# A two-layer hybrid decoder trunk: sixteen weight rests formed by adding DMAs instead of VectorE

## The chip, the cores and the metric

The kernel runs on one core of one Trainium2 chip. The metric is the device time of one execution in microseconds; the time before is the median of three runs. All views of the profile come from one profiled execution.

## The reference

The reference is a decoder trunk of two layers over 512 tokens of width 1024, in float32.

```
for i in range(2):
    h = rms_norm(x, mix_norm[i])
    if i == 0:  x = x + attention_and_short_conv(h)      # one input, one output projection
    else:       x = x + gla_mixer(h)                     # chunked gated linear attention
    x = x + conv_ffn(rms_norm(x, ffn_norm[i]))           # 1024 -> 2 x 2816 -> 1024
    x = x + sigmoid(rms_norm(x, ple_norm[i]) @ w_gate[i]) * (p[i] @ w_proj[i])
```

Two places matter here. In the GLA mixer, `h @ w_in` has 1024 value columns (and 16 columns of a low-rank gate beside them). The last line of the second layer is the end of the program: a gate of 1024 x 1024 weights, a projection of 256 x 1024 weights, a sigmoid, a product, a sum, and the output.

## The kernel before

Every matrix product is made from three float32r products: each operand is split into a high part (a float32r copy) and a rest (the value less the high part), and `mm3` issues high x high, high x rest of the right operand, and rest of the left x high, in this order, on lines 153, 154 and 155. For a weight the high part is `wh` and the rest `wl`. In the two stages of this study the weights are the right operand, the tokens' columns the left one, so line 154 reads `wl`.

Weights come through `weights` or, in the last stage, through `raw` and `cut` directly. A load is issued on SyncE's queue into one of two `raw` buffers (128 x 2048 float32 at most). `cut` divides the loaded piece into two halves when it has more than 1024 elements for each partition, either by columns (`by="b"`) or by blocks of rows (`by="a"`). In the second way a half is one contiguous row in each partition. For each half ScalarE copies the values to `wh` (line 133), and VectorE subtracts: `wl = raw - wh` (line 134). There are three buffers each for `wh` and `wl` in the general pool, so a half is cut when TensorE has finished with the half three before it. A raw buffer is free for the next load when the last reader of it, the subtraction, is done.

The order on each engine is fixed when the program is built: a scheduler goes through the instructions by the order of the program as their inputs come ready in its own model of time. On the chip each engine then runs its list in order.

**GLA's values** (`mixer1`, class `Values`). The value columns are made in three groups: columns 672 to 1040 (352 values and the 16 gate columns), 0 to 336 and 336 to 672. Each group has two loads, of four blocks of 128 rows each, and each load is cut in two halves: four pieces for a group, of 128 x 672 in the two groups with 336 columns. `step(0)` and `step(1)` run the products of the two loads over the four token tiles. The second and third groups stand in the midst of the decays and scores of the four heads, which fill VectorE and ScalarE with short instructions; the three groups' products are independent of those.

**The last stage** (`ple1`). `load(hf, ...)` loads the gate weights of one half of the output columns (`hf` 0 or 1), as two loads of four row blocks by 512 columns, each cut into two pieces of 128 x 1024. In this text B0 to B3 are the four pieces of the first half, C0 to C3 those of the second. The first half uses the general pool with three buffers, the second a pool of its own with four. The first half's products run over k outermost, for all four token tiles at once (each piece feeds 24 products); then come the projection weights, the transposes of `p` (`pT`, split into `ph` and `pl`), the second half's gate weights, the second projection weights, the transposes of the residual (`back`, copied by ScalarE to `xt`), and for each token tile the finish of the first half and the products and the finish of the second, where each piece feeds six products for one tile. `finish` multiplies ScalarE's sigmoid `so` by the projection and adds `xt`.

Loads are issued on SyncE's queue in the order of its list, here: first half's two gate loads, first projection weights, second half's two gate loads, second projection weights.

Of the kernel before, what the change touches and what calls it, by code (L numbers as in the profile page):

```python
# [9 lines left out]
F32 = mybir.dt.float32  # L10
# [3 lines left out]
AF = mybir.ActivationFunctionType  # L14
ALU = mybir.AluOpType
# [40 lines left out]
class Kernel:  # L56
# [45 lines left out]
                out=l, in0=src, scalar=gain, in1=h.bitcast(F32), op0=ALU.mult, op1=ALU.subtract  # L102
            )

    def weights(self, src, na, nb, by="b"):
        raw = self.raw(na, nb)
        self.nc.sync.dma_start(raw, src)
        return self.cut(raw, by)

    def raw(self, na, nb):  # L110
        t = self.wp.tile([P, 2048], F32, tag="raw", name=self.nm("raw"), bufs=2)
        return t[:, : na * nb].rearrange("p (a b) -> p a b", b=nb)

    def cut(self, rv, by, pool=None, bufs=3):


        nc = self.nc
        pool = pool or self.wp
        na, nb = rv.shape[1:]
        parts = []  # L120
        n = 2 if na * nb > 1024 else 1
        for k in range(n):
            if by == "b":
                a, b = na, nb // n
                v = rv[:, :, k * b : (k + 1) * b]
            else:
                a, b = na // n, nb
                v = rv[:, k * a : (k + 1) * a, :]
            h = pool.tile([P, 1024], F32R, tag="wh", name=self.nm("wh"), bufs=bufs)
            l = pool.tile([P, 1024], F32R, tag="wl", name=self.nm("wl"), bufs=bufs)  # L130
            hv = h[:, : a * b].rearrange("p (a b) -> p a b", b=b)
            lv = l[:, : a * b].rearrange("p (a b) -> p a b", b=b)
            nc.scalar.activation(hv, v, AF.Copy)  # L133
            nc.vector.tensor_tensor(lv, v, hv.bitcast(F32), ALU.subtract)  # L134
            parts.append((hv, lv))

        def get(i, c0, c1):
            if by == "b":
                b = nb // n
                k = c0 // b  # L140
                h, l = parts[k]
                return h[:, i, c0 - k * b : c1 - k * b], l[:, i, c0 - k * b : c1 - k * b]
            a = na // n
            h, l = parts[i // a]
            return h[:, i % a, c0:c1], l[:, i % a, c0:c1]

        return get
# [622 lines left out]
    def ple1(self):  # L770

        nc, a, tc = self.nc, self.a, self.tc
        xg, r = self.xg, self.r
        wg = a["ple_w_gate"][1].rearrange("(k p) n -> p k n", p=P)
        wp = a["ple_w_proj"][1].rearrange("(k p) n -> p k n", p=P)
        sl = lambda hl, t: (hl[0][:, t * P : (t + 1) * P], hl[1][:, t * P : (t + 1) * P])
        with tc.tile_pool(name="ple1", bufs=1) as fp:

            def load(hf, pool, bufs):
                ws = []  # L780
                for k0 in (0, 4):
                    raw = self.raw(4, 512)
                    nc.sync.dma_start(raw, wg[:, k0 : k0 + 4, hf * 512 : hf * 512 + 512])
                    ws.append(self.cut(raw, "a", pool, bufs))
                return lambda k, c0, c1: ws[k // 4](k % 4, c0, c1)

            def back(hf, t):

                pb = self.pa()
                for q in range(4):  # L790
                    nc.tensor.transpose(
                        pb[:, q * P : (q + 1) * P], self.xT[4 * hf + q][:, t * P : (t + 1) * P], self.ident
                    )
                x = fp.tile([P, 512], F32, tag="xt", name=self.nm("xt"), bufs=8)
                nc.scalar.copy(x, pb)
                return x

            def finish(hf, t, pg, x, w, c0=0, c1=512):
                n = c1 - c0
                pj = self.pa()  # L800
                for k in range(2):
                    self.mm3(pj[:, :n], sl(pT[k], t), w(k, c0, c1), start=k == 0, stop=k == 1)
                s = fp.tile([P, 512], F32, tag="so", name=self.nm("so"), bufs=4)[:, :n]
                nc.scalar.activation(s, pg, AF.Sigmoid, scale=r[:, t : t + 1])
                nc.vector.tensor_tensor(s, s, pj[:, :n], ALU.mult)
                nc.vector.tensor_tensor(s, s, x[:, c0:c1], ALU.add)
                nc.sync.dma_start(self.out[0, t * P : (t + 1) * P, hf * 512 + c0 : hf * 512 + c1], s)

            w = load(0, self.wp, 3)
            pgs = [self.ps() for _ in range(NT)]  # L810
            for k in range(ND):
                for t in range(NT):
                    self.mm3(pgs[t], sl(xg[k], t), w(k, 0, 512), start=k == 0, stop=k == ND - 1)
            wj = self.weights(wp[:, :, :512], 2, 512, by="a")
            pT = self.load_p(1, fp)
            w = load(1, fp, 4)
            wj1 = self.weights(wp[:, :, 512:], 2, 512, by="a")
            x0 = [back(0, t) for t in range(NT)]
            x1 = [back(1, t) for t in range(NT)]
            for t in range(NT):  # L820
                finish(0, t, pgs[t], x0[t], wj)
                cuts = (0, 512) if t < NT - 1 else (0, 256, 512)
                for c0, c1 in zip(cuts, cuts[1:]):
                    pg = self.ps()[:, : c1 - c0]
                    for k in range(ND):
                        self.mm3(pg, sl(xg[k], t), w(k, c0, c1), start=k == 0, stop=k == ND - 1)
                    finish(1, t, pg, x1[t], wj1, c0, c1)


    def mixer1(self):  # L830
        nc, a, tc = self.nc, self.a, self.tc
        xg, r = self.xg, self.r
        w_in = a["gla_w_in"][0].rearrange("(k p) n -> p k n", p=P)
        tok = lambda k, t: (xg[k][0][:, t * P : (t + 1) * P], xg[k][1][:, t * P : (t + 1) * P])
        with tc.tile_pool(name="m1", bufs=1) as mp:
# [5 lines left out]
            class Values:  # L841


                def __init__(v, c0, c1, vn):
                    v.c0, v.n, v.vn = c0, c1 - c0, vn
                    v.ws = [
                        self.weights(w_in[:, k0 : k0 + 4, 1024 + c0 : 1024 + c1], 4, v.n, by="a") for k0 in (0, 4)
                    ]

                def step(v, i):  # L850
# [288 lines left out]
            v = Values(672, 1040, 352)  # L1139
# [40 lines left out]
            v = Values(0, 336, 336)  # L1180
# [7 lines left out]
            v = Values(336, 672, 336)  # L1188
# [93 lines left out]
```

## Time and profile before

| what | before |
|---|---|
| median of three runs | 1260.85 us (1260.66 to 1261.68) |
| the profiled execution | 1260.71 us |
| its span, first to last instruction | 1258.8 us |
| granted TensorE clock | 0.999 |
| TensorE busy | 1244.9 us, 99% |
| VectorE busy | 772.7 us, 61% |
| ScalarE busy | 541.1 us, 43% |
| GpSimd busy | 54.1 us, 4% |
| rests on VectorE (line 134) | 222, 258.6 us |
| high parts on ScalarE (line 133) | 222, 224.7 us |
| gate loads of 1024 KB, issue to landing | 5.0 us (median) |

How to read it: busy time is the time in which an engine ran instructions; matmuls are pipelined, so a product of 512 columns shows some 0.39 us while the next begins 0.227 us after it. `PE` is TensorE, `PEld` its weight load, `DVE` VectorE, `ACT` ScalarE, `POOL` GpSimd, `SP` SyncE; a name with a q is the queue that issues DMAs. In a timeline's line stand the start and the duration in us, the engine and the line of the kernel, the operation, the tiles written and read, the shape, the count of merged instructions, and in brackets the idle time before it with what ended it. `ps` and `pa` are the PSUM banks, four of each.

### The profile page before, as it was taken

To read this page: it belongs to the slowest core of one execution; us is meant where nothing else is said; L and a number is where in the kernel's file an instruction comes from. 1 tells how busy PE (TensorE), PEld (TensorE's weight loads), DVE (VectorE), ACT (ScalarE), POOL (GpSimd) and SP (SyncE) were. 2 spreads that over 40 slices of the span, in tenths; PEclk is the share of its full clock that TensorE was granted. 3 is DMA by queue.
4 is the path that set the end of the run, shared out by engine and by line. 5 is a ranking of instruction groups with operands and counts; after the bars stand their busy time and mean duration, and the time that the engine had idled before them with its cause. 6 is when DMAs were issued, how large, how long until landed. Compare 5 with 4: busy or idle time off the path is not lost.

```text
span 1258.8 us, 14853 instructions
## 1 busy us (share of the span) xinstructions
PE 1244.9 (99%) x5851; PEld 1038.1 (82%) x5851; DVE 772.7 (61%) x1190; ACT 541.1 (43%) x831; POOL 54.1 (4%) x150
## 2 busy tenths in 40 slices
PE   7999999999999999999999999999999999999998
PEld 7777788888888888888989988888888888888887
DVE  6776566777777633346679765557777777433343
ACT  6456344444444422234563544335444444232341
POOL 2500000000000000000100000000000000000000
PEclk9999999999999999999999999999999999999999
DMA  6221232333332233223322222333222233222331
GB/s 212 73 76 55 79 99 93 100 101 101 100 100 92 76 111 99 92 74 101 109 89 67 68 68 67 100 100 102 98 88 86 98 100 101 92 92 93 108 107 61
DMA packets 110473, 117.42 MB, mean 93 GB/s; under 512 B 2712, under 2 KB 105682, under 8 KB 110404
## 3 DMA queue, kind: packets, MB, share of 16 engines
q1 hardware_dynamic: 108512, 114.83, 28.0%
q10 hardware_dynamic: 1332, 1.23, 0.3%
q8 instruction: 46, 0.75, 0.2%
q0 software_dynamic: 560, 0.42, 0.2%
q14 instruction: 23, 0.19, 0.0%
HBM read 114.37 MB, written 2.10 MB: 93 GB/s over the span
## 4 chain that ended last, share of the span: by engine, by line
PE 92%; DVE 3%; ACT 2%; issue 1%; POOL 1%; DMA 1%; SPq 0%; DVEq 0%; POOLq 0%; ACTq 0%
PE ps L153 28%; PE ps L155 28%; PE ps L154 28%; PE pa L492 1%; PE pa L1001 1%; DMA xin<-in_x_dram 1%; PE pa L1115 1%; PE pa L154 1%; DVE wl L134 1%; PE pa L153 1%; PE pa L155 1%; PE pa L538 1%; PE pa L1092 0%; POOL rq L163 0%; PE pa L1117 0%
## 5 line engine op out<-in xcount | busy, mean ns | idle before, releaser
L133 ACT ACTIVATE wh<-raw 128x1024 fp32r<-128x1024 f32 (+4 forms) x222 | 224.7, 1015 | 384.5 <-PE ps L154 319.4
L134 DVE TENSOR_TENSOR wl<-raw,wh 128x1024 fp32r<-128x1024 f32 (+4 forms) x222 | 258.6, 1167 | 184.0 <-ACT wh L133 182.9
L153 PE MATMUL ps<-a,wh 128*128 128x512 f32 x864 | 337.4, 390 | 0.0
L154 PE MATMUL ps<-a,wh 128*128 128x512 f32 x864 | 337.0, 390 | 0.0
L155 PE MATMUL ps<-a,wl 128*128 128x512 f32 x864 | 336.8, 390 | 0.0
L153 PEld LDWEIGHTS ps<-a,wh 128*128 128x128 f32 x864 | 162.5, 188 | 34.3 <-issue 0.7
L155 PEld LDWEIGHTS ps<-a,wl 128*128 128x128 f32 x864 | 162.5, 188 | 34.0 <-issue 0.2
L154 PEld LDWEIGHTS ps<-a,wh 128*128 128x128 f32 x864 | 162.5, 188 | 33.8 <-issue 0.3
L682 DVE SCALAR_TENSOR_TENSOR zt<-z,vfa,zt 128x512 f32<-128x512 f32 x176 | 131.4, 749 | 3.6 <-ACT zt L680 0.6
L153 PE MATMUL ps<-b,wh 128*128 128x512 f32 x320 | 126.3, 396 | 0.6 <-ACT b L97 0.5
L155 PE MATMUL ps<-b,wl 128*128 128x512 f32 x320 | 125.3, 392 | 0.0
L154 PE MATMUL ps<-b,wh 128*128 128x512 f32 x320 | 124.9, 391 | 0.0
L679 DVE TENSOR_TENSOR z<-ps,R 128x512 f32<-128x512 f32 x88 | 60.4, 688 | 74.7 <-PE ps L155 74.7
L153 PE MATMUL ps<-ah,wh 128*128 128x512 f32 x224 | 87.1, 389 | 0.0
L154 PE MATMUL ps<-al,wh 128*128 128x512 f32 x224 | 87.1, 389 | 0.0
L155 PE MATMUL ps<-ah,wl 128*128 128x512 f32 x224 | 87.1, 389 | 0.0
L680 ACT ACTIVATE zt<-z,vfb 128x512 f32<-128x512 f32 x88 | 70.9, 807 | 5.0 <-DVE z L679 3.3
L153 PEld LDWEIGHTS ps<-b,wh 128*128 128x128 f32 x320 | 60.0, 188 | 14.0 <-ACT b L97 1.3
L155 PEld LDWEIGHTS ps<-b,wl 128*128 128x128 f32 x320 | 60.1, 188 | 12.5
L154 PEld LDWEIGHTS ps<-b,wh 128*128 128x128 f32 x320 | 60.1, 188 | 12.2
L704 ACT ACTIVATE zt<-zt 128x512 f32<-128x512 f32 x44 | 27.8, 631 | 74.8 <-DVE zt L682 74.8
L299 DVE TENSOR_TENSOR xT<-xT,ps 128x512 f32<-128x512 f32 x32 | 22.0, 688 | 57.4 <-PE ps L155 57.4
(290 smaller groups left out, 1506.1 us busy)
## 6 DMA issues: line engine op xcount, KB each, us to landing
raw<-in_ffn_w_up_dram SPq DMA_DIRECT2D x44, 1024.0 KB, 5.0
raw<-in_ffn_w_down_dram SPq DMA_DIRECT2D x16, 1024.0 KB, 5.1
raw<-in_hy_w_in_dram SPq DMA_DIRECT2D x8, 1024.0 KB, 5.0
raw<-in_ple_w_gate_dram SPq DMA_DIRECT2D x8, 1024.0 KB, 5.0
raw<-in_gla_w_in_dram SPq DMA_DIRECT2D x8, 1024.0 KB, 5.3
raw<-in_ffn_w_down_dram SPq DMA_DIRECT2D x8, 768.0 KB, 4.3
raw<-in_gla_w_out_dram SPq DMA_DIRECT2D x4, 1024.0 KB, 5.0
raw<-in_gla_w_in_dram SPq DMA_DIRECT2D x4, 672.0 KB, 4.0
```

Of the source, the lines that this page charges most:

```text
L133: nc.scalar.activation(hv, v, AF.Copy)
L134: nc.vector.tensor_tensor(lv, v, hv.bitcast(F32), ALU.subtract)
L153: mm(out, lh, rh, start=start, stop=False)
L154: mm(out, lh, rl, start=False, stop=False)
L155: mm(out, ll, rh, start=False, stop=stop)
L299: self.nc.vector.tensor_tensor(self.xT[m], self.xT[m], ps, ALU.add)
L492: nc.tensor.matmul(pb[:, hh * 256 : hh * 256 + w], qTs[t][64 * g : 64 * g + 64, hq, :], kT[64 * g : 64 * g + 64, k0 : k0 + w], start=True, ...
L538: nc.tensor.transpose(pb[:, hh * P : (hh + 1) * P], s[:, 4 * g + hh, c * P : (c + 1) * P], self.ident)
L679: nc.vector.tensor_tensor(z[:, 2:], ps, R, ALU.mult)
L680: nc.scalar.activation(y, z[:, 2:], AF.Identity, scale=w2[:, f : f + 1], bias=bb[:, f : f + 1])
L682: nc.vector.scalar_tensor_tensor(out=y, in0=z[:, tap : tap + S], scalar=w[:, f : f + 1], in1=y, op0=ALU.mult, op1=ALU.add)
L704: nc.scalar.activation(y, y, AF.Gelu)
```

## The change

`cut` gets an argument `added`. Where it is set, VectorE's subtraction is replaced by two steps: ScalarE makes a second, negated copy of the values into `wl`, rounded to float32r as the first one is, so that `wl` holds minus the high part; and a DMA issued by GpSimd adds the raw values to it in place (`accum_op=ALU.add`). Both sides of the DMA are flattened, so that each partition's row is contiguous: 672 or 1024 elements, 2688 or 4096 bytes.

It is set for the gate weights in `ple1` (both calls of `load`, eight pieces of 512 KB) and for the two groups of GLA's values with 336 columns (eight pieces of 336 KB). The other 206 pieces are cut as before.

```diff
-    def weights(self, src, na, nb, by="b"):
+    def weights(self, src, na, nb, by="b", added=False):
         raw = self.raw(na, nb)
         self.nc.sync.dma_start(raw, src)
-        return self.cut(raw, by)
+        return self.cut(raw, by, added=added)
...
-    def cut(self, rv, by, pool=None, bufs=3):
+    def cut(self, rv, by, pool=None, bufs=3, added=False):
...
             nc.scalar.activation(hv, v, AF.Copy)
-            nc.vector.tensor_tensor(lv, v, hv.bitcast(F32), ALU.subtract)
+            if added:
+
+                nc.scalar.activation(lv, v, AF.Copy, scale=-1.0)
+                flat = lambda x: x.rearrange("p a b -> p (a b)")
+                nc.gpsimd.dma_start(flat(lv), flat(v), accum_op=ALU.add)
+            else:
+                nc.vector.tensor_tensor(lv, v, hv.bitcast(F32), ALU.subtract)
...
-                    ws.append(self.cut(raw, "a", pool, bufs))
+                    ws.append(self.cut(raw, "a", pool, bufs, added=True))
...
-                        self.weights(w_in[:, k0 : k0 + 4, 1024 + c0 : 1024 + c1], 4, v.n, by="a") for k0 in (0, 4)
+                        self.weights(w_in[:, k0 : k0 + 4, 1024 + c0 : 1024 + c1], 4, v.n, by="a", added=c0 != 672)
+                        for k0 in (0, 4)
```

## The prediction

> **What bounds the kernel now.** I read the page's busy times first, then the table of busy time by stretch for the two stages that are touched, then the waits, and last the timelines of ScalarE, SyncE's queue and TensorE in the last stage.
>
> ```profile
> PE 1244.9 (99%) x5851; PEld 1038.1 (82%) x5851; DVE 772.7 (61%) x1190; ACT 541.1 (43%) x831; POOL 54.1 (4%) x150
> ```
> ```profile
> core 0: us, PE busy (x) PEld busy (x) DVE busy (x) ACT busy (x) POOL busy (x), PEclk, DMA share, GB/s
> ...
> 640.00:700.00 60.00, 59.92 (x354) 52.72 (x353) 52.70 (x118) 29.32 (x51) 2.75 (x2) 1.00 0.19 59
> 700.00:780.00 80.00, 79.88 (x446) 69.59 (x446) 52.69 (x115) 38.47 (x87) 5.69 (x7) 1.00 0.22 70
> ...
> 1186.00:1232.00 46.00, 45.98 (x228) 38.48 (x227) 20.30 (x24) 20.76 (x28) 1.01 (x1) 1.00 0.27 95
> ```
>
> TensorE is the bound everywhere. In the 140 us around GLA it is idle 0.2 us, in the 46 us of the last stage 0.02 us, at a granted clock of 1.00. Of its 13.9 idle us in the span, 7.2 lie in the first 12 us and 3.7 after 1232. VectorE, which the change relieves, is 53 of 60 us busy in GLA's first stretch, but TensorE loses nothing to it. So almost nothing can be won; what can be lost is TensorE's time, wherever a rest `wl` lands late.
>
> **What an added DMA takes.** No DMA that adds, and none from SBUF to SBUF, is in this trace. The nearest rows (issue to landing):
>
> ```profile
> raw<-in_ple_w_gate_dram SPq DMA_DIRECT2D x8, 1024.0 KB, 5.0
> ...
> raw<-in_ple_w_proj_dram SPq DMA_DIRECT2D x2, 512.0 KB, 3.5
> ...
> vrow<-in_ffn_conv_w_dram POOLq DMA_DIRECT2D x6, 22.0 KB, 2.0
> ```
>
> Call X the time from the end of the negated copy to the landing of a 512 KB add. Below: as a plain 512 KB load, 3.5 us. Two streams (`raw` and `wl` both read): 1024 KB, 5.0. Three streams (and `wl` written) at the 1.5 us per 512 KB between these rows: 6.5. Above: four times the plain row's 1.5 us per 512 KB of variable part in rows that don't overlap, 2.0 + 8 = 10 (two reads, an add and a write in sequence, with some loss). I take 6.5: all three streams are there, GpSimd must issue it (a GpSimd issue takes 0.52 us here), and weight loads are in flight beside it. For GLA's 336 KB pieces the same three streams are 1008 KB, 5.0 us. All 16 issues stand on GpSimd's queue, 16 x 0.52 = 8.3 us on an engine busy for 4%; behind them are only the `rsqrt` powers and small copies, and a power of 1.0 us at 1200.24 is not needed before the first sigmoid at 1218.
>
> **GLA's values.** Removed: 8 VectorE rests of 0.85 us, 6.8 us. Added: 8 ScalarE copies at 0.76 (the 128x672 row), 6.1 us, on an engine 29 of 60 us busy, and 8 adds. ScalarE's exponentials of the decays queue behind a copy by 0.76 at most; VectorE's relief gives as much back. Each add must land before the second product of its piece. The tightest is the fourth piece of the first group: its copy starts at 686.65 (a buffer comes free only then), both copies end at 688.1, TensorE reads its `wl` at 694.41: 6.3 us, against 5.0. The others have 8.6 and more. A raw buffer is now held until the add has landed: 5.0 + 0.76 instead of 0.85 us, some 5 later per second piece, but the next load is used 9 us or more afterwards. Sum here: 0.
>
> **The last stage.** Removed: 8 rests of 1.23 us on VectorE, which is 44% busy here. Added: 8 ScalarE copies (1.0 each back to back) and 8 adds of 512 KB.
>
> ```profile
> 1186.30 1.06 ACT L133 ACTIVATE wh<-raw 128x1024 fp32r<-128x1024 f32 x1 [4.59 <-PE ps L154]
> ...
> 1201.11 1.06 ACT L133 ACTIVATE wh<-raw 128x1024 fp32r<-128x1024 f32 x1 [4.41 <-PE ps L155]
> ...
> 1208.38 2.01 ACT L133 ACTIVATE wh<-raw 128x1024 fp32r<-128x1024 f32 x2 [0.76 <-DMA raw<-in_ple_w_gate_dram]
> 1213.92 2.96 ACT L133 ACTIVATE wh<-raw 128x1024 fp32r<-128x1024 f32 x3 [3.53 <-DMA raw<-in_ple_w_gate_dram]
> 1216.90 1.28 ACT L804 ACT_TABLE_LOAD   x1
> 1218.19 0.69 ACT L804 ACTIVATE so<-ps,rtok 128x512 f32<-128x512 f32 x1
> 1218.78 1.08 ACT L97 ACTIVATE ph<-pa 128x512 fp32r<-128x512 f32 x2
> 1219.74 4.14 ACT L795 COPY xt<-pa 128x512 f32<-128x512 f32 x8
> ```
> ```profile
> 1219.27 0.39 PE L154 MATMUL ps<-wl,a 128*128 128x512 f32 x1
> ...
> 1227.62 0.39 PE L154 MATMUL ps<-wl,a 128*128 128x512 f32 x1
> ```
>
> The reader sees two waits for a buffer freed by TensorE (first half's gate weights, pieces B0 and B3), then two for loads (second half's, C0 to C3), then a packed run of ScalarE; and, in TensorE's rows, the first use of C0's rest and the first of C3's.
>
> First half: B0's two copies end at 1186.30 + 2.0 = 1188.3 and its rest is read at 1194.71: 6.4 us, against X 6.5, so nothing or 0.1. B1, B2 and B3 have 8.7, 10.0 and 8.9 (first reads at 1201.08, 1206.54, 1211.98).
>
> Second half: there are two raw buffers, and this is where the cover ends. B3's two copies end at 1203.1; its raw buffer is free at 1203.1 + X instead of 1203.46, when C0's load is issued in SyncE's order. The load takes 4.9 to its copy: C0 and C1 are copied from 1208.1 + X, four copies in 3.9, so their adds land at 1210.1 + 2X and 1212.0 + 2X. C2's load follows C0's in SyncE's queue and is there before ScalarE gets to it; with the two `ph` copies (1.08) between, C2's rest is there at 1215.1 + 2X, C3's at 1217.1 + 2X. X counts twice. With 6.5:
> - C0's rest at 1223.1, first read at 1219.27: 3.8 late in this order.
> - C3's at 1230.1, first read at 1227.62: 2.5 late.
> - ScalarE begins C0 at 1214.6 instead of 1208.38. From there it has 8 copies (7.9), the projection weights (1.06), the table load, the first sigmoid, `ph` and the eight `xt` copies: 16.2 us, to 1230.8, where the last ended at 1223.9: 6.9 late. TensorE waits for the sigmoid (it frees a PSUM bank) and for `xt` (its transposes' banks).
>
> These overlap, they don't add: the loss lies between 2.5 and 6.9, and TensorE can move some transposes and projections ahead of the products that wait. I take 5.0, near the middle and above C0's 3.8. At the other ends: with X at 3.5 C3's rest is at 1224.1, in time, loss 0 if the sigmoid isn't queued behind the copies, 2.7 if it is (eight copies then end at 1219.5, and load and sigmoid of 1.97 follow: 1221.5 against 1218.88); with 10, below.
>
> The profiled execution took 1260.71 us, a span of 1258.8 and 1.9 around it, and lies 0.14 under the median of 1260.85. Sum: 1260.7 + 0 + 5.0 = **1265.7**.
>
> **Rivals.**
> *Hidden (0.27).* X is 4.4 or less and the sigmoid keeps its place ahead of the late copies. For it: the 512 KB row's 3.5; C3 at 1217.1 + 8.8 = 1225.9 is in time. Against: a longer ScalarE queue just where it was packed. Time 1260.7, at most some 2 more: not slower. It decides at X = 5.3, where C3 meets 1227.62. The Trainium skill speaks for this one: DMA: Bandwidth & Descriptors, "Anatomy of one DMA — SWDGE (gpsimd) path", gives 2.0 us plus bytes at 436 GB/s, and Collectives: The Full Stack, "The bandwidth ceiling: the fold count and why AG ≠ RS ≠ AR", says that an add costs its second read and no cycles of its own; an estimate from both is 2.0 + 2.4 = 4.4 us, and the sum by it would be 1260.7. The 1024 KB row, 5.0 with one read, is 0.6 above that estimate.
>
> *The order holds (0.16).* The projection weights' copy stands ahead of the table load on ScalarE (the third of the x3 row). Its load needs C1's raw buffer, free at 1225.0: +3.5, +1.06, and then 1.97 for table and sigmoid: 1231.5 instead of 1218.88. Transposes wait for `ph` and `xt` behind it, so all 12.6 is lost: 1273.3.
>
> *The adds crawl (0.12).* X = 10: B0's rest is 3.6 late, B3's another 1.1 (its buffer is freed later, and its copies end at 1206.7), C3's at 1240.7 against 1227.62 + 4.7, 8.4 more; in GLA, at 8 us for 336 KB, the fourth piece is 1.7 late. Together 14.8: 1275.5. Nothing in the trace excludes it, and nothing shows it.
>
> *Faster (0.03).* VectorE's chain in GLA is shortened by 6.8 us, but TensorE's idle time there is 0.2 us: 1260.5. More than 0.2% needs time that only the ends have.
>
> **How the numbers follow.** The forecast holds 0.42. 0.2% is 2.5 us, about what a measurement of this kernel can tell from no change. The forecast, the held order and the crawl are slower by more: 0.42 + 0.16 + 0.12 = 0.70; hidden is the same, 0.27; 0.03 faster. The range goes from 1259.9 (hidden, with some relief) to 1276 (crawl); what is left out is adds slower than 10 us, and a gain above 0.8. The forecast's own range, X from 5.5 to 7.5 at two us for each, is 1263.7 to 1267.7.
>
> **What would show it.** VectorE's rests fall from 222 to 206, ScalarE's line 133 keeps 222 beside 16 new copies. The adds' median landing is X without the copy's hand-over: right at 6, wrong below 4.5 or above 8. The first-half gate products start without a gap; TensorE idles 4 to 6 us between 1219 and 1232, waiting for a DMA into `wl` or for ScalarE's `so` or `xt`; C0's load is issued near 1209.6 instead of 1203.46. GLA's value products show no gap. An idle TensorE in GLA, or none in the last stage, would make the forecast wrong.

## The result and the profile after

The changed kernel takes 1271.58 us (median of four runs, 1270.78 to 1273.48), the kernel before 1260.76 beside it: ratio 1.0089 (1.0077 to 1.0101), 10.8 us slower. The forecast was 5.0 slower.

The profiled execution is the slowest of the four: 1273.48 us, a span of 1271.7, 12.8 above the profile of before. Some 1.5 us of this is lost before 200 us of the span (the granted clock was 0.84 between 50 and 70 us, against 0.91: the same wait of 2.2 us is followed by 6.8 us at half the clock here and by 3.4 before), and the last stage begins 1.5 later on this trace's axis. The rest is in the last stage: from the transposes of `p` to TensorE's last matmul it took 49.0 us, against 37.66 before, so 11.3 longer. This stretch is called the tail below.

The busy times and the group of VectorE's rests, from the page of after:

```profile
PE 1250.9 (98%) x5851; PEld 1041.9 (82%) x5851; DVE 757.1 (60%) x1174; ACT 553.7 (44%) x847; POOL 68.2 (5%) x166
...
L140 DVE TENSOR_TENSOR wl<-raw,wh 128x1024 fp32r<-128x1024 f32 (+3 forms) x206 | 242.2, 1176 | 181.1 <-ACT wh L133 180.1
```

Sixteen rests are gone from VectorE and sixteen instructions are new on ScalarE and on GpSimd. The table by stretch (columns as in the one of before) says where it cost TensorE something:

```profile
640.00:700.00 60.00, 59.96 (x346) 52.53 (x344) 47.42 (x111) 33.28 (x56) 8.06 (x8) 1.00 0.35 80
700.00:780.00 80.00, 79.85 (x452) 69.36 (x451) 51.53 (x112) 40.34 (x91) 7.53 (x9) 1.00 0.29 83
...
1186.00:1232.00 46.00, 39.94 (x188) 33.01 (x186) 6.76 (x10) 23.23 (x28) 8.03 (x9) 0.95 0.78 194
```

Around GLA TensorE is idle 0.19 us of 140, as before. In the last stage it is idle 6.06 of 46, and the mean granted clock there falls from 1.00 to 0.95. The DMA issues, with the median from issue to landing:

```profile
wl<-raw POOLq DMA_DIRECT2D x8, 512.0 KB, 5.5
...
wl<-raw POOLq DMA_DIRECT2D x8, 336.0 KB, 4.3
...
raw<-in_ple_w_proj_dram SPq DMA_DIRECT2D x2, 512.0 KB, 8.3
```

The last row holds the landing of the first of the two projection loads alone: 8.3 with adds in flight, 3.5 before. The second, on which the end of the stage hangs, has no landing on record; it took 7.4 from its issue to its copy. How that reaches TensorE is seen in three timelines of after. ScalarE's:

```profile
1214.53 1.06 ACT L133 ACTIVATE wh<-raw 128x1024 fp32r<-128x1024 f32 x1 [5.35 <-DMA raw<-in_ple_w_gate_dram]
...
1222.12 1.06 ACT L97 ACTIVATE ph<-pa 128x512 fp32r<-128x512 f32 x2
1223.08 1.07 ACT L801 COPY xt<-pa 128x512 f32<-128x512 f32 x2
1224.16 1.28 ACT L810 ACT_TABLE_LOAD   x1
1225.45 0.69 ACT L810 ACTIVATE so<-ps,rtok 128x512 f32<-128x512 f32 x1
1231.72 1.06 ACT L133 ACTIVATE wh<-raw 128x1024 fp32r<-128x1024 f32 x1 [5.58 <-DMA raw<-in_ple_w_proj_dram]
1232.68 3.21 ACT L801 COPY xt<-pa 128x512 f32<-128x512 f32 x6
```

SyncE's queue:

```profile
1209.36 1.47 SPq L789 DMA_DIRECT2D raw<-in_ple_w_gate_dram  x2
1224.36 0.37 SPq L107 DMA_DIRECT2D raw<-in_ple_w_proj_dram  x1
```

TensorE's:

```profile
1223.47 2.99 PE L797 MATMUL pa<-cf,xT 128*128 128x128 f32 x16 [2.81 <-DVE pl L98]
...
1228.35 0.40 PE L159 MATMUL ps<-wh,a 128*128 128x512 f32 x1
1233.30 1.97 PE L797 MATMUL pa<-cf,xT 128*128 128x128 f32 x8 [4.55 <-ACT xt L801]
...
1235.50 0.63 PE L160 MATMUL pa<-wl,ph 128*128 128x512 f32 x1
1235.92 0.63 PE L161 MATMUL pa<-wh,pl 128*128 128x512 f32 x1
```

Three things follow one another. First, the eight copies of C0 to C3 fill ScalarE to 1222.1; `ph` and `pl` come after them, and TensorE waits 2.81 for `pl`. Second, the second projection weights wait for a raw buffer until C1's add has landed (issued at 1224.36; at 1211.86 before, on an axis that is 1.5 earlier), their load takes 7.4 to its copy, and ScalarE stands at that copy for 5.58 with six `xt` copies behind it: TensorE waits 4.55. Third, the products after that wait follow each other at 0.42 to 0.43 us until 1237.6, not at 0.227. Busy time by 5 us, clock in the third column from the right:

```profile
1220.00:1225.00 5.00, 2.19 (x18) 1.95 (x16) 1.29 (x2) 4.98 (x8) 1.72 (x2) 0.92 1.05 204
1225.00:1230.00 5.00, 3.75 (x14) 2.80 (x12) 0.00 (x0) 1.13 (x2) 0.00 (x0) 0.73 1.02 182
1230.00:1235.00 5.00, 1.70 (x9) 1.70 (x9) 1.23 (x1) 3.28 (x6) 0.00 (x0) 0.61 0.19 73
1235.00:1240.00 5.00, 5.00 (x18) 4.04 (x17) 1.38 (x2) 0.78 (x2) 0.00 (x0) 0.71 0.02 3
```

So of the 11.3 us, 7.4 are two waits and some 4.0 are a TensorE that runs at a lower clock after them (worked out below, in the part on the clock). No wait of TensorE for a DMA into `wl` is in this trace.

### The profile page after: what moved, and what is told of

It is laid out like the page before. It is cut to its first block, busy times and chain, and to the rows that moved or that the text cites. A ratio compares the mean times of both kernels' runs of the same rounds, so it can differ in the third digit from the quotient of the medians.

```text
span 1271.7 us, 14892 instructions
## 1 busy us (share of the span) xinstructions
PE 1250.9 (98%) x5851; PEld 1041.9 (82%) x5851; DVE 757.1 (60%) x1174; ACT 553.7 (44%) x847; POOL 68.2 (5%) x166
## 4 chain that ended last, share of the span: by engine, by line
PE 92%; DMA 3%; issue 2%; DVE 1%; ACT 1%; POOL 1%; SPq 0%; DVEq 0%; POOLq 0%; ACTq 0%
PE ps L159 28%; PE ps L161 28%; PE ps L160 28%; PE pa L1008 1%; PE pa L498 1%; DMA wl<-raw 1%; DMA xin<-in_x_dram 1%; DMA raw<-in_ple_w_proj_dram 1%; PE pa L1122 1%; PE pa L161 1%; PE pa L544 1%; PE pa L160 1%; PE pa L159 1%; PE pa L1099 0%; DMA raw<-in_ple_w_gate_dram 0%
## 5 line engine op out<-in xcount | busy, mean ns | idle before, releaser
L140 DVE TENSOR_TENSOR wl<-raw,wh 128x1024 fp32r<-128x1024 f32 (+3 forms) x206 | 242.2, 1176 | 181.1 <-ACT wh L133 180.1
```

## The experiments

Theories: **queue** (what costs is the two raw buffers held by adds, and ScalarE's list behind late loads), **late rest** (a product reads a `wl` that hasn't landed), **ScalarE's load** (sixteen more copies are too many), **traffic** (the adds slow other transfers wherever they run), and, from the first runs on, **clock** (an idle TensorE is slow afterwards). The table gives all runs against the kernel before beside them; the tail's change, the waits and the last column are from each run's trace. The last column is half of the time in which TensorE was busy at half its clock, also explained below.

| kernel | median us | ratio (95%) | tail | TensorE's waits in the tail | lost at half clock |
|---|---|---|---|---|---|
| after | 1271.58 | 1.0089 (1.0077 to 1.0101) | +11.3 | 2.81 `pl`, 4.55 `xt` | 4.0 |
| gla_only | 1261.62 | 1.0007 (0.9997 to 1.0016) | 0.0 | none | 0 |
| first_half | 1264.19 | 1.0023 (1.0014 to 1.0032) | +4.2 | 1.52 `so`, 1.20 `xt` | 1.4 |
| second_half | 1267.97 | 1.0054 (1.0039 to 1.0069) | +8.0 | 0.61 `so`, 4.69 `xt` | 2.6 |
| own_buffer | 1265.94 | 1.0038 (1.0023 to 1.0053) | +4.9 | 3.16 `pl` | 1.7 |
| add_vector | 1262.36 | 1.0016 (1.0007 to 1.0025) | +1.7 | 0.97 `xt`, 0.47 `so` | 0 |
| neg_vector | 1270.58 | 1.0077 (1.0060 to 1.0094) | +10.2 | 8.02 `xt` | 2.1 |
| own_buffer_neg_vector | 1262.29 | 1.0012 (1.0003 to 1.0022) | +1.8 | 0.92 `so`, 0.71 `pl` | 0 |
| second_half_filled | 1267.60 | 1.0057 (1.0042 to 1.0072) | +7.4 | 0.72 `xt` | 0 |
| plain_copy | 1262.12 | 1.0009 (1.0000 to 1.0019) | +1.0 | 0.76 `so` | 0 |
| proj_first | 1265.93 | 1.0040 (1.0025 to 1.0055) | +6.1 | 2.83 `so`, 0.30 DMA into `wl` | 3.0 |

### Which part of the change

**gla_only**: GLA's adds stay, the last stage is as before.

```diff
-                    ws.append(self.cut(raw, "a", pool, bufs, added=True))
+                    ws.append(self.cut(raw, "a", pool, bufs))
```

> The adds of GLA's values only (8 of 336 KB); the last stage as before. Queue theory (the whole loss is in the last stage: ScalarE's list, run in order, is held by the second projection weights' copy, whose load waits for a raw buffer until an add has landed): 1260.8, no loss. Late-rest theory (a `wl` that lands after TensorE wants it): also 1260.8, since the tightest piece has 6.3 us and these adds took 4.3. Traffic theory (adds and loads slow each other on the DMA engines, wherever they are): 1262 to 1264, with gaps in the value products.

1261.62, 1.0007 (0.9997 to 1.0016): no loss is shown. From the sums of GLA's norm (at 616.41 us) to those of the norm behind it (838.04) the trace has 221.6 us, as before (616.00 and 837.62). The traffic theory is out for GLA.

**first_half** and **second_half**: adds for B0 to B3 alone, or for C0 to C3 alone; GLA as before.

```diff
-                    ws.append(self.cut(raw, "a", pool, bufs, added=True))
+                    ws.append(self.cut(raw, "a", pool, bufs, added=hf == 0))    # second_half: hf == 1
...
-                        self.weights(w_in[:, k0 : k0 + 4, 1024 + c0 : 1024 + c1], 4, v.n, by="a", added=c0 != 672)
+                        self.weights(w_in[:, k0 : k0 + 4, 1024 + c0 : 1024 + c1], 4, v.n, by="a", added=False)
```

> Adds only for the first half's gate pieces B0 to B3. Queue theory: the raw buffer of B2 and B3 is freed some 5 us later, the second half's loads start later, and the second projection weights' load with them; ScalarE is held for about 2 to 3 us ahead of the residual's copies: 1263 to 1264. ScalarE-load theory (the extra copies themselves are the loss): the four copies of B lie where ScalarE waits, 1260.8. Late-rest theory: B's rests are in time, 1261 at most.

> Adds only for the second half's gate pieces C0 to C3; the first half by VectorE. The second half's loads start as before (1203.5 us on the time axis of before). Queue theory: C1's add lands at about 1217.5 instead of VectorE's rest at 1211.8, the second projection weights come some 5 us later and hold ScalarE: 1264 to 1266. ScalarE-load theory: four extra copies of 0.95, two of them where ScalarE had waited: 1262 to 1263. Late-rest theory: the adds land by 1223, in time: 1260.8 to 1261.

Each half alone costs: 3.6 and 7.4 us by the medians, together about what the change costs. In first_half nothing of the first half waits; the loss comes when C0's load is issued at 1207.18 instead of 1203.46, so that the sigmoid ends late. second_half lost more than was expected, and this is where the projection weights came into view. Its ScalarE:

```profile
1225.06 1.06 ACT L133 ACTIVATE wh<-raw 128x1024 fp32r<-128x1024 f32 x1 [4.95 <-DMA raw<-in_ple_w_proj_dram]
```

and its TensorE:

```profile
1226.64 3.67 PE L797 MATMUL pa<-cf,xT 128*128 128x128 f32 x16 [4.69 <-ACT xt L801]
```

Here the sigmoid and `ph` ran almost in time, and still one copy that waits for a load holds the eight `xt`. The load was issued at 1218.30, where before it was at 1211.86.

### Buffer, copies and addition apart

**own_buffer**: the second projection weights get a raw tile of their own (paid for with one of the `so` buffers), so their load waits for no add.

```diff
-                s = fp.tile([P, 512], F32, tag="so", name=self.nm("so"), bufs=4)[:, :n]
+                s = fp.tile([P, 512], F32, tag="so", name=self.nm("so"), bufs=3)[:, :n]
...
-            wj1 = self.weights(wp[:, :, 512:], 2, 512, by="a")
+            rj = fp.tile([P, 1024], F32, name="rj").rearrange("p (a b) -> p a b", b=512)
+            nc.sync.dma_start(rj, wp[:, :, 512:])
+            wj1 = self.cut(rj, "a")
```

> The changed kernel, with the second projection weights loaded into a buffer of their own (and three `so` buffers instead of four to make room), so that their load waits for no add. Queue theory: TensorE's second wait (4.6 us) goes, and part of the time at the lower clock with it: 1264 to 1266. ScalarE-load theory: no gain, 1270 to 1271.6. Late-rest theory: no gain, since C's adds land when they did.

1265.94, as the queue theory had it: the wait for `xt` is gone and so are 5.6 of the 10.8 us. What is left is 3.16 us for `pl`, behind the eight copies, and 1.7 at half the clock after it.

**add_vector**: in the last stage VectorE makes the addition; ScalarE still makes both copies.

```diff
-                nc.gpsimd.dma_start(flat(lv), flat(v), accum_op=ALU.add)
+                if nb == 336:
+                    nc.gpsimd.dma_start(flat(lv), flat(v), accum_op=ALU.add)
+                else:
+                    nc.vector.tensor_tensor(lv, v, lv.bitcast(F32), ALU.add)
```

> The changed kernel with the last stage's eight adds done by VectorE (the negated copies stay on ScalarE); GLA's adds stay DMAs. It keeps ScalarE's extra copies and takes the DMAs' landing time out of the raw buffers' hold. Queue theory (raw buffers held until an add lands, then a load, then ScalarE in order): the buffers come free about 1 us later than before instead of 6, the second projection weights are there when ScalarE gets to them: 1261.5 to 1263. ScalarE-load theory (the extra copies are the loss): 1266 or more.

1262.36: with all the copies of the change on ScalarE the loss is 1.7 us, in which TensorE waits 0.97 for `xt` and 0.47 for `so`. The copies aren't what costs, unless they begin late.

**neg_vector**: the other way round: VectorE makes the negated copies of the last stage, the DMAs add.

```diff
-                nc.scalar.activation(lv, v, AF.Copy, scale=-1.0)
+                if pool is None and nb == 336:
+                    nc.scalar.activation(lv, v, AF.Copy, scale=-1.0)
+                else:
+                    nc.vector.tensor_scalar_mul(lv, v, -1.0)
```

> The changed kernel with the last stage's eight negated copies on VectorE instead of ScalarE; the adds stay DMAs. ScalarE's list has the sigmoid and `ph` ahead again, but the second projection weights' copy stands ahead of seven of the eight `xt` copies and still waits for its load. Queue theory: TensorE's first wait (2.8 us) goes, the second (4.6 us) stays or grows by what the first took: 1266 to 1270. ScalarE-load theory: the loss goes, 1261 to 1262.

1270.58: nearly the whole loss, with ScalarE no busier in the last stage than before. Its ScalarE and its TensorE (the line numbers are 3 higher here):

```profile
1227.49 1.06 ACT L133 ACTIVATE wh<-raw 128x1024 fp32r<-128x1024 f32 x1 [7.78 <-DMA raw<-in_ple_w_proj_dram]
```
```profile
1229.07 2.82 PE L800 MATMUL pa<-cf,xT 128*128 128x128 f32 x12 [8.02 <-ACT xt L804]
```

The first wait (`pl`) has gone with the copies, but the second has grown from 4.55 to 8.02: whoever comes earlier to the projection weights waits longer there.

**own_buffer_neg_vector**: the last two edits together.

> Both: the second projection weights in a buffer of their own and the last stage's negated copies on VectorE; the sixteen adds stay DMAs. Queue and ScalarE theories together: both waits are gone, 1260.8 to 1262. Late-rest theory: C's loads still start some 6 us late (raw buffers held by B's adds), so C's rests land at about 1222 to 1228 and TensorE waits for one of them, at a line that names a DMA into `wl`: 1263 to 1266.

1262.29, just above what the queue theory gave, with 1.6 us of waits in the tail, all short, and a clock that stays at 1.00. The adds are still DMAs here, of 6.0 us in the median, and no product waits for one. So late rests are no part of the loss; the queue on ScalarE and the held raw buffer are, and they can be taken away one by one.

### The clock

**second_half_filled**: second_half with 27 products of zeros, accumulated into a bank in use, where TensorE waits for `xt`.

```diff
+            def fill(n):
+                for _ in range(n):
+                    nc.tensor.matmul(pgs[3], sl(xg[0], 3)[0], zr, start=False, stop=False)
...
-            x0 = [back(0, t) for t in range(NT)]
+            x0 = []
+            for t in range(NT):
+                x0.append(back(0, t))
+            fill(27)
```

> The run with adds for C only, and 27 more products of a zero operand (6.1 us) added to the last token tile's gate sums, placed where TensorE waited 4.7 us for `xt`; seven useful products that had stood in that place come 1.6 us later. Clock theory (the granted clock falls because TensorE idles, and the products behind a wait are slow for it): the clock stays 1.00 after the wait, the products behind it come every 0.23 us instead of 0.43, and in spite of the 1.6 us the time is 1266 to 1267.5 against 1268.0. If the clock falls for another reason (traffic, phase of the program), the clock after the wait is still 0.5 to 0.8 and the time 1269 to 1270.

1267.6, not faster: the filling takes 27 x 0.227 = 6.1 us in a place where TensorE had waited 4.7 and had done seven useful products, 1.6 us of work, which now come behind it. But the clock is what was asked. The 5 us around the end of the wait, in second_half:

```profile
1225.00:1230.00 5.00, 3.36 (x17) 3.36 (x17) 1.23 (x1) 4.57 (x8) 0.00 (x0) 0.50 0.01 3
```

and in second_half_filled:

```profile
1225.00:1230.00 5.00, 4.28 (x27) 3.37 (x26) 1.36 (x2) 4.46 (x9) 0.00 (x0) 1.00 0.02 3
```

With TensorE kept at work, the clock is not lowered, though the same adds and loads ran just before. It is the idling that lowers it.

Read on finer stretches, the granted clock in these tails is 1.00 or 0.50, never between, and it changes only at edges that lie 3.41 us, or a multiple of it, apart; the means over 5 us mix the two. In after, cut at these edges:

```profile
1220.83:1224.24 3.41, 0.77 (x7) 0.77 (x8) 1.29 (x2) 3.39 (x7) 1.50 (x2) 1.00 1.00 193
1224.24:1227.65 3.41, 3.41 (x15) 2.99 (x14) 0.00 (x0) 1.89 (x2) 0.00 (x0) 0.50 1.10 210
1227.65:1231.07 3.42, 1.10 (x5) 0.57 (x3) 0.00 (x0) 0.00 (x0) 0.00 (x0) 1.00 0.92 210
1231.07:1234.48 3.41, 1.18 (x6) 1.18 (x7) 1.23 (x1) 2.76 (x5) 0.00 (x0) 0.50 0.01 2
1234.48:1237.89 3.41, 3.41 (x11) 2.83 (x10) 0.02 (x1) 1.30 (x3) 0.00 (x0) 0.50 0.03 5
```

TensorE idles 2.64 us of the first stretch and 2.32 of the third, and the clock is 0.50 behind each of them; behind a stretch without a wait it is 1.00 again. Work at half the clock takes twice as long, so half of TensorE's busy time there is lost: (3.41 + 1.18 + 3.41) / 2 = 4.0 us. Waits and this loss together give the change of the tail to within 0.3 us in every run (in second_half_filled with the 28 products of zeros, 6.4 us, beside them); in second_half 5.3 + 2.6 make 7.9 of 8.0. Of the stretches at 1.00 in the tails, those with 2.06 us of waits or more were followed by half the clock (2.06 in first_half), those with 1.49 or less were not. Near 1.9 the traces have both: 1.91 in neg_vector left the clock at 1.00, 1.88 near 62 us in after lowered it.

### What the addition itself costs

**plain_copy**: the sixteen DMAs copy `raw` to `wl` and add nothing; the instructions on ScalarE and TensorE keep their order.

```diff
-                nc.gpsimd.dma_start(flat(lv), flat(v), accum_op=ALU.add)
+                nc.gpsimd.dma_start(flat(lv), flat(v))
```

> The changed kernel with sixteen plain copies from `raw` to `wl` in place of the adds: the addition is left out, so `wl` holds the values themselves; issue, queue and bytes written are the same. If an add costs its second read (the 512 KB adds took 5.5 us, with all DMA engines busy at some 210 GB/s), a copy runs at nearly twice that rate, lands in 4 to 4.5 us, and the buffers come free 1 to 1.5 us sooner, twice in the chain: 1268 to 1270. If the addition costs nothing beside a copy: 5.5 us, 1271 to 1272.

1262.12, 1.0009 (1.0000 to 1.0019): an expectation that missed by 6 us at its nearer end. Its DMA issues:

```profile
wl<-raw POOLq DMA_DIRECT2D x8, 512.0 KB, 2.9
...
wl<-raw POOLq DMA_DIRECT2D x8, 336.0 KB, 2.7
```

A DMA without the addition lands 2.6 us earlier for 512 KB. It counts twice. The C loads are issued at 1207.06 instead of 1209.36 (this trace's axis is 0.2 behind that of after), the projection weights' at 1219.10 instead of 1224.36, 5.3 us earlier; and no adds slow that load, so its copy begins at 1223.58 with no wait. TensorE waits 0.76 in the tail, and the clock stays at 1.00. By the medians the 16 more ScalarE copies and the 16 DMA issues of the change cost some 1.2 us, at the edge of what the runs can tell from nothing. The other 9.5 hang on the addition: 2.6 us in each transfer, the load that is slower beside adds, and the waits and the clock that follow; this run takes all of it away at once and doesn't weigh the parts.

**proj_first**: the second projection weights are loaded and cut ahead of C0 to C3.

```diff
-            w = load(1, fp, 4)
             wj1 = self.weights(wp[:, :, 512:], 2, 512, by="a")
+            w = load(1, fp, 4)
```

> The changed kernel with one line moved: the second projection weights are loaded and cut ahead of the second half's gate weights. Queue theory: their copy no longer stands between the sigmoid and the `xt` copies, but they take the raw buffer that B's add frees, so C2 and C3 are loaded only after their cut, and the copies of C2 and C3 stand ahead of all eight `xt` copies: the hold moves, it does not go. 1266 to 1270. If only the place of the second projection weights' copy in ScalarE's list mattered: 1264 to 1266, as with a buffer of their own.

1265.93, at the border of the two expectations, so it tells neither from the other. The wait has moved: the copies of C0 and C1 begin only at 1215.03 us, the sigmoid stands behind them, and TensorE waits 2.83 for `so`; the copies of C2 and C3 follow behind the sigmoid and `ph`, ahead of the eight `xt` copies. This is also the only kernel where it waits for a late rest, 0.30 us.

## Why the prediction was right or wrong

**Right.** The sign, and GLA at nothing: the adds took 4.3 us in the median and 6.7 at most, TensorE waited for none, and gla_only shows no loss. The first half without a gap: all 6.06 idle us of the stretch are the two waits of the tail. The chain through the two raw buffers: the C loads were issued at 1209.36 (1209.6 was forecast) and the copies began at 1214.53 (1214.6). That the times agree is luck, since this trace runs 1.5 late: on the axis of before the loads came 1.8 earlier than forecast. From the end of the negated copy to the buffer's release were 5.9 us, both for B3 and for C1, where X was taken as 6.5, and B3's negated copy ran ahead of its plain one and so ended 1.2 sooner than assumed. plain_copy shows that the time of the add, counted twice, is the heart of it.

**The estimate from the Trainium skill** was 4.4 us for the add. The row that it was weighed by, 6.5 from three streams, was 0.6 above the 5.9 that were measured, the estimate 1.5 below. What the Trainium skill says in Collectives: The Full Stack, "The bandwidth ceiling: the fold count and why AG ≠ RS ≠ AR", that an add costs its second read, agrees in kind: the share of the DMA engines that the queue of these transfers took went from 1.8% without the addition to 3.2% with it, for the same bytes. By the Trainium skill's DMA: Bandwidth & Descriptors, "Anatomy of one DMA — SWDGE (gpsimd) path", a 512 KB copy would take an estimated 3.2 us; 2.9 were measured.

**Wrong: the step "these overlap … I take 5.0".** It has three faults.

The late rests of C0 and C3 (3.8 and 2.5) were read off the order of before. The scheduler put the products of the second half later, and no run but proj_first waits for a rest. These terms were nothing.

The term of ScalarE's queue was right in kind and became the first wait, 2.81 for `pl`. What was missing is the second: the projection weights' copy. The rival *The order holds* named this copy, the buffer that it waits for, and its time (C1's buffer at 1225.0; the load was issued at 1224.36, on an axis that is 1.5 later), but weighed it only with the copy ahead of the sigmoid, for 12.6. It stands behind the sigmoid and ahead of six `xt` copies, where it costs 4.55. And its load was taken at 3.5, as in the trace of before; with the adds of C2 and C3 in flight it took 7.4. So two of the cases came in part at once, though they were priced as exclusive. own_buffer (5.6 us back) and neg_vector (8.02 in one wait) show it.

The clock was in no term. The sum took a TensorE that is late to be late by its waits; here 7.4 us of waits became 11.3. The runs agree: waits under 1 us left the clock at 1.00 (plain_copy, add_vector, own_buffer_neg_vector), waits of 1.52 and 1.20 close together (first_half) and the longer ones of the other runs brought it to 0.50 for 3.4 or 6.8 us, and filling the wait kept it up. The Trainium skill has a rule for this in TensorE: Matmul & The Clock Gate, "What's actually happening": after about 3.4 us of idling the array gets half its clock, and after as much work the whole one. The half agrees with the pitch of the products after the wait, 0.43 against 0.227, and the 3.4 us with the 3.41 between the edges; but 2.06 us of waits in such a stretch (first_half) were enough here, less than the time stated there. By the rule a wait that is long enough costs an estimated 1.7 us more (3.4 at half the clock). The one of own_buffer cost 1.7; the two of after cost 4.0, since the second was followed by twice 3.41 us at half the clock.

Smaller slips moved nothing: 1203.1 and the load's 4.9 make 1208.0 and not 1208.1, 1221.5 is 2.6 and not 2.7 behind 1218.88, and the 8 us in the upper bound of X are two more than four times 1.5, which the prediction puts down to loss; the slowest of the 512 KB adds took 7.9.

**Open.** At how much idling between 1.5 and 2.1 us in a stretch the clock falls, and how much it takes to keep it down, isn't settled. That a third raw buffer would take away the loss is argued from own_buffer; it wasn't tried. What plain_copy and add_vector lose lies in their tails (1.0 and 1.7). The 1.0 us by which gla_only's median lies above the kernel before does not: some 0.5 of it is outside the span from first to last instruction (2.5 us there against 1.9), and its cause is open; the run can't tell it from nothing.

## What to carry to other kernels

Price a slower step by the time for which it holds its buffers, and multiply that by the number of loads that pass through them in a row before the end: 2.6 us in each transfer became 9.5 here, with the waits and the clock that followed. Then go down the list of the engine that copies from those buffers and ask of each waiting instruction what stands behind it, with loads priced beside the new traffic and not as they were without it. And where TensorE is the bound, a wait of some microseconds is paid again in its clock, here with a quarter of its length (neg_vector) to nearly the whole (proj_first).

## What the runs showed of the hardware

- A DMA from SBUF to SBUF that adds takes 5.5 us for 512 KB in rows of 4096 bytes and 4.3 for 336 KB in rows of 2688 (medians); one that copies takes 2.9 and 2.7. GpSimd is held 0.86 us to issue an adding one, 0.53 for a copy.
- While adds run alone the 16 DMA engines are full at some 210 GB/s of counted bytes (1220 to 1225 above, where the next load is issued only at 1224.36: share 1.05, 204 GB/s), and a 512 KB load beside them took 7.4 us to its copy; the first projection weights' took 8.3 to its landing, 3.5 without adds.
- The clock granted to TensorE in the last stage was 1.00 or 0.50, changing at edges 3.41 us or a multiple apart. It was 0.50 for 3.41 or 6.83 us after a stretch with 2.06 us of waits or more, and the loss was half of TensorE's busy time at 0.50 (1.4 to 4.0 us).
